# Attention scores: the low-key product with 64 rows of high query only, two heads in the two halves of the TensorE array

## The chip, the core and the metric

The kernel runs on one core of a Trainium2 chip. The metric is the device time of one launch in microseconds (us). Before the change the median of three runs is 2594.91 us (2594.48 to 2594.93).

## The reference

One encoder layer is applied to a prompt of 512 tokens and a sample of 256 tokens (width 2048), with shared weights. What the change touches is the windowed attention: 16 query heads of 64 channels in 4 groups, each group sharing one of 4 key/value heads, after a rotary turn. Each block of 128 queries sees its own key block and its neighbours.

```python
def window_attention(q, k, v, sink):
    ...
    scale = HEAD_DIM ** -0.5
    s = jnp.einsum('bnqhgd,bnkhd->bnhgqk', qb, kb).astype(jnp.float32) * scale
    ...
    s = jnp.where(valid[None, :, None, None, :, :], s, NEG_INF)
    m = jnp.maximum(jnp.max(s, axis=-1, keepdims=True), sink_l)
    p = jnp.exp(s - m)
    p = p / (jnp.sum(p, axis=-1, keepdims=True) + jnp.exp(sink_l - m))
    o = jnp.einsum('bnhgqk,bnkhd->bnqhgd', p.astype(v.dtype), vb)
```

Around it stand an RMSNorm and the input projection, a 2-D Fourier mix of the other 1024 channels, the output projection `w_out`, and a squared-ReLU MLP of width 8192.

## The kernel before

Every float32 product is made from two parts of each factor: a high part (the value as TensorE's one-pass float32 format, `F32R`, holds it) and a low part (the rest). A product is then high times high, high times low and low times high.

The program runs in stages: the input projection with the Fourier mix (to about 378 us of the trace), then a stage that interleaves the attention with the output projection (378 to about 735 us), then the two MLP products (lines 1187 and 1622), which fill the rest.

In the attention stage TensorE's order is written out by hand. The output projection is the ground beat: a step is one pass through `proj_slot` for one `k`, three matmuls of 512 columns (line 1040), and `run_events` is called after each step. The attention work is hung into this beat through a heap of events, `at(t, fn)`, with `t` in steps. TensorE's instructions are placed so, and the DMA issues on SP and the work of VectorE, ScalarE and GpSimd stand in the same order in their own queues.

The attention itself is cut into 24 units, `units[u] = (b, g)`: six query blocks `b` by four head groups `g`, with four heads `h` each. A unit begins every `pace` = 7.37 steps. For one head, `qk` (line 839) makes the scores `s` (128 queries by `nk` keys; `nk` is 256 in the 16 units of blocks 0, 3, 4 and 5, and 384 in the 8 units of blocks 1 and 2). `row_max` (VectorE, line 863) adds the mask, takes the maximum and writes the masked scores into `p`, which frees the PSUM buffer of `s`; there are three such buffers. Then come `exps` (ScalarE), `normalize` (GpSimd, line 893), `trans` (four transposes on TensorE, line 905) and `pv` (line 924).

A tile `qs` holds a unit's queries: rows 0 to 63 the high part, rows 64 to 127 the low part, for four heads. `kdh` and `kdl` hold the high and the low keys, each twice, in the upper and in the lower 64 rows. So one matmul with `kdh` over 128 rows gives (high + low query) times high key, and one with `kdl` gives (high + low query) times low key. That is two matmuls a head, 192 in all. The heads' events are `d_qk` = 1.73 steps apart; `row_max` follows 0.4 step after `qk`.

`load_q(u)` (line 724) brings `qs` from two scratch tensors in HBM, `qr_d[g][0]` (high) and `qr_d[g][1]` (low), with two DMA issues on SP. `qs` has two buffers, so the load for unit `u + 2` waits until the scores of unit `u` are done. Other issues on the same queue bring the weights of the output projection (`raw`) and the Fourier results (`ofr`).

Of the kernel before, what the change touches and what calls it, by code (L numbers as in the profile page):

```python
# [12 lines left out]
F32R = mybir.dt.float32r  # L13
# [7 lines left out]
P = 128  # L21
# [11 lines left out]
HD = 64  # L33
# [7 lines left out]
def hybrid_encoder(ctx: ExitStack, tc: tile.TileContext, a: dict):  # L41
    nc = tc.nc
    ctx.enter_context(tc.manual_schedule(engines={mybir.EngineType.PE}))

    def f32(ap):
        return ap.bitcast(F32)
# [71 lines left out]
    qr_d = [[dpool.tile([2 * P, T], F32, tag=f"q{c}{i}", name=f"q{c}{i}") for c in "hl"] for i in range(NKV)]  # L118
# [60 lines left out]
    def load_of(m, tiles=None):  # L179

        of_raw[m] = tiles or [
            op.tile([P, FG, P], F32, tag=f"of{'hl'[m - 1]}-1", name="ofr")
            if m < 3 else ap_.tile([P, FG, P], F32, tag="ofr", name="ofr", bufs=2)
        ]
        for i, raw in enumerate(of_raw[m]):
            k = raw.shape[1]
            src = of_d[i * k * P : (i + 1) * k * P, m * P : (m + 1) * P]
            nc.sync.dma_start(raw[:], src.rearrange("(k p) t -> p k t", p=P))
# [9 lines left out]
    with ExitStack() as ph:  # L198
# [456 lines left out]
        kt = {}  # L655
# [65 lines left out]
        units = [(b, g) for b in range(NM) for g in range(NKV)]  # L721
        state = {}

        def load_q(u):
            b, g = units[u]
            t0 = slice(b * P, (b + 1) * P)
            qs = kt["kp"].tile([P, 4, P], F32R, tag="qs", name="qs", bufs=2)
            state[u] = {"qs": qs}
            for o in range(2):
                nc.sync.dma_start(f32(qs[o * HD : (o + 1) * HD]), qr_d[g][o][:, t0].rearrange("(d h) t -> d h t", h=4))  # L730

        todo = {}

        def after(piece, fn):
            todo.setdefault(piece, []).append(fn)
# [20 lines left out]
            after(14.5 + i, lambda i=i: load_k(i))  # L756
        for u in range(2):
            after(18 + 0.5 * u, lambda u=u: load_q(u))
        after(18, lambda: load_of(0, [kt["kp"].tile([P, 4, P], F32, tag="zy", name="ofr", bufs=2) for _ in range(2)]))
        n_in = 4 * len(cols)  # L760
        in_raw, in_w = {}, {}
# [26 lines left out]
        for piece in range(n_in):  # L788
# [7 lines left out]
            for c in range(2):  # L796
                cs = slice(c * P, (c + 1) * P)
                for i in range(4):
                    first, stop = j == 0 and i == 0, j == 3 and i == 3
                    for w, o, n in ((wh, 0, 0), (wh, 1, 1), (wl, 0, 2)):  # L800
                        for s in range(2):
                            nc.tensor.matmul(  # L802
                                ps[c][s][:, :HALF], w[:, i, cs], whole[j // 2][s][o][:, 4 * (j % 2) + i, :],
                                start=first and n == 0, stop=stop and n == 2,
# [28 lines left out]
    mask, sink, kdh, kdl = (kt[c] for c in ("mask", "sink", "kdh", "kdl"))  # L833

    def key_blocks(b):
        lo, hi = (0, 3) if b < 4 else (4, 5)
        return max(lo, b - 1), min(hi, b + 1)

    def qk(u, heads):
        b, g = units[u]  # L840
        k0, k1 = key_blocks(b)
        nk = (k1 - k0 + 1) * P
        st = state[u]
        for h in heads:
            s = tiles.pop("s", None) or pp3.tile([P, 512], F32, tag="s", name="s", bufs=3)
            st[f"s{h}"] = s
            for n, kd in enumerate((kdl, kdh)):
                nc.tensor.matmul(s[:, :nk], st["qs"][:, h, :], kd[:, g, k0 * P : k0 * P + nk], start=(n == 0), stop=(n == 1))  # L848

    def row_max(u, heads):  # L850
        b, g = units[u]
        k0, k1 = key_blocks(b)
        nk = (k1 - k0 + 1) * P
        off = (k0 - b + 1) * P
        st = state[u]
        if heads[0] == 0:
            for x, w in (("mx", 4), ("nm", 4), ("rs", 4), ("es", 4), ("p", 4 * 384)):
                st[x] = ap_.tile([P, w], F32, tag=x, name=x)
            st["p"] = st["p"][:].rearrange("p (h k) -> p h k", h=4)
        mx = st["mx"]  # L860
        for h in heads:
            s = st[f"s{h}"]
            nc.vector.tensor_tensor_reduce(
                out=st["p"][:, h, :nk], in0=s[:, :nk], in1=mask[:, off : off + nk], scale=1.0,
                scalar=sink[:, 4 * g + h : 4 * g + h + 1], op0=ALU.add, op1=ALU.max, accum_out=mx[:, h : h + 1],
            )
        hs = slice(heads[0], heads[-1] + 1)
        nc.vector.tensor_scalar(out=st["nm"][:, hs], in0=mx[:, hs], scalar1=-1.0, scalar2=None, op0=ALU.mult)
        if heads[-1] == 3:
            nc.vector.tensor_tensor(out=st["es"][:], in0=sink[:, 4 * g : 4 * g + 4], in1=mx[:], op=ALU.subtract)  # L870

    def exps(u, heads):
        b, g = units[u]
        k0, k1 = key_blocks(b)
        nk = (k1 - k0 + 1) * P
        st = state[u]
        for h in heads:
            nc.scalar.activation(
                st["p"][:, h, :nk], st["p"][:, h, :nk], AF.Exp, bias=st["nm"][:, h : h + 1],
                accum_out=st["rs"][:, h : h + 1],  # L880
            )
        if heads[-1] == 3:
            nc.scalar.activation(st["es"][:], st["es"][:], AF.Exp)

    def normalize(u):
        k0, k1 = key_blocks(units[u][0])
        nk = (k1 - k0 + 1) * P
        st = state[u]
        rs, es, p = st["rs"], st["es"], st["p"]
        nc.vector.tensor_tensor(out=rs[:], in0=rs[:], in1=es[:], op=ALU.add)  # L890
        nc.vector.reciprocal(out=rs[:], in_=rs[:])
        for h in range(4):
            nc.gpsimd.tensor_scalar(
                out=p[:, h, :nk], in0=p[:, h, :nk], scalar1=rs[:, h : h + 1], scalar2=1.0, op0=ALU.mult, op1=ALU.mult
            )
        st["pt"] = {}

    def trans(u, kb):
        st = state[u]
        k0, k1 = key_blocks(units[u][0])  # L900
        if k0 + kb > k1:
            return
        pt = tiles.pop("t", None) or pp3.tile([P, 512], F32, tag="t", name="t", bufs=3)
        for h in range(4):
            nc.tensor.transpose(pt[:, h * P : (h + 1) * P], st["p"][:, h, kb * P : (kb + 1) * P], ident[:])  # L905
        th = ap_.tile([P, 512], F32R, tag="th", name="th", bufs=4)
        tl = ap_.tile([P, 512], F32R, tag="tl", name="tl", bufs=4)
        later(t_th, lambda: nc.scalar.activation(th[:], pt[:], AF.Copy))
        later(t_tl, lambda: nc.vector.tensor_tensor(out=tl[:], in0=pt[:], in1=f32(th[:]), op=ALU.subtract))
        st["pt"][kb] = (th, tl)  # L910
# [73 lines left out]
    pace, t_first, t_qk, d_qk, t_max, t_exp, t_norm = 7.37, 4, -4.5, 1.73, 0.4, 2.65, 3.65  # L984
# [6 lines left out]
    def at(t, fn):  # L991
        clock[1] += 1
        heapq.heappush(events, (t, clock[1], fn))
# [8 lines left out]

    for u in range(len(units)):
        t = pace * u + t_first
        for h in range(4):
            dt = t_qk + d_qk * h
            at(t + dt, lambda u=u, h=h: qk(u, (h,)))
            at(t + dt + t_max, lambda u=u, h=h: row_max(u, (h,)))
            at(t + dt + t_exp, lambda u=u, h=h: exps(u, (h,)))
        at(t + t_norm, lambda u=u: normalize(u))  # L1010
        if u + 2 < len(units):
            at(t + t_lq + 2 * (u == 1), lambda u=u: load_q(u + 2))
        for kb in range(3):
            at(t + t_trans + d_trans * kb, lambda u=u, kb=kb: trans(u, kb))
            at(t + t_pv + d_pv * kb, lambda u=u, kb=kb: pv(u, kb))
# [117 lines left out]
    units = [(0, g) for g in range(NG)] + [(1, g) for g in (NG - 1, *range(NG - 1))]  # L1133
# [672 lines left out]
```

## Time and profile before

| | us |
|---|---|
| median of the three runs | 2594.91 |
| the profiled execution, its own time | 2593.48 |
| span of that execution | 2591.6 |
| TensorE busy in the span | 2576.9 |
| VectorE busy | 1810.9 |
| ScalarE busy | 1124.4 |
| GpSimd busy | 266.3 |
| attention interleaved with the output projection, from the first to the last score matmul | 378.2 to 577.5 |

PE is the matmul side of TensorE and PEld its weight load, which runs beside it; DVE is VectorE, ACT ScalarE, POOL GpSimd, SP the queue that issues most DMAs. The length that the profile gives a matmul reaches past the start of the next one, since matmuls are pipelined. What a matmul costs in a row of matmuls is therefore read from start to start, here called its slot.

### The profile page before, as it was taken

What the parts mean: (1) busy time and instruction counts of PE and PEld (TensorE: products, weight loads), DVE (VectorE), ACT (ScalarE), POOL (GpSimd) and SP (SyncE); (2) the same over time, 40 slices, a digit from 0 to 9 for tenths busy, and PEclk for the clock granted to TensorE, in tenths of its full rate; (3) what the DMA queues carried; (4) which work ended last, traced back from release to release, by engine and by line L of the source; (5) the groups of instructions that cost most, each with busy time, mean ns of one, the idle gap of its engine ahead of it and who ended that gap; (6) DMA issues with size and microseconds to landing.
All of it is one profiled execution on the core that took longest, in us unless ns stands there. A gap on an engine that the chain in (4) does not pass through costs nothing.

```text
span 2591.6 us, 34972 instructions
## 1 busy us (share of the span) xinstructions
PE 2576.9 (99%) x13580; PEld 2359.3 (91%) x13580; DVE 1810.9 (70%) x2208; ACT 1124.4 (43%) x1574; POOL 266.3 (10%) x367
## 2 busy tenths in 40 slices
PE   9999999999999999999999999999999999999998
PEld 9999998888899999999999999988888888888887
DVE  7966567777655656556777877767776765777687
ACT  6545437674334333333444454433333333333335
POOL 1001333233210101000000000110000000000000
PEclk9999999999999999999999999999999999999999
DMA  7863385345664445456666766675543662555364
GB/s 251 311 225 113 127 240 175 117 131 193 216 202 159 163 157 187 161 191 236 212 216 227 232 215 213 240 306 176 184 153 112 219 235 82 179 179 164 98 207 155
DMA packets 268998, 489.54 MB, mean 189 GB/s; under 512 B 19568, under 2 KB 164000, under 8 KB 267424
## 3 DMA queue, kind: packets, MB, share of 16 engines
q1 hardware_dynamic: 197328, 321.26, 39.2%
q10 hardware_dynamic: 58688, 115.18, 11.7%
q0 software_dynamic: 12816, 50.87, 5.8%
q8 instruction: 107, 1.75, 0.3%
q14 instruction: 59, 0.48, 0.1%
HBM read 360.35 MB, written 126.88 MB: 188 GB/s over the span
## 4 chain that ended last, share of the span: by engine, by line
PE 96%; DVE 1%; DMA 1%; ACT 1%; issue 0%; POOL 0%; SPq 0%; DVEq 0%; POOLq 0%; ACTq 0%
PE pu L1187 36%; PE pd L1622 35%; PE pm L1040 10%; PE pz L802 5%; PE p L268 4%; PE o L924 1%; PE t L905 1%; PE s L848 1%; PE pv L391 1%; PE ptx L137 0%; PE pe L630 0%; PE pa L609 0%; DMA raw<-in_w_in 0%; DMA zf<-zf 0%; PE pt L137 0%
## 5 line engine op out<-in xcount | busy, mean ns | idle before, releaser
L1187 PE MATMUL pu<-xf,wh 128*128 128x384 f32 x3072 | 780.2, 334 | 0.0
L1187 PEld LDWEIGHTS pu<-xf,wh 128*128 128x128 f32 x3072 | 554.0, 188 | 1.5 <-ACT o L1205 1.3
L1622 PE MATMUL pd<-wl,sh 128*128 128x512 f32 x1332 | 517.7, 389 | 0.0
L1622 PE MATMUL pd<-wh,sh 128*128 128x512 f32 x1332 | 517.7, 389 | 0.0
L1622 PE MATMUL pd<-wh,sl 128*128 128x512 f32 x1332 | 517.5, 389 | 0.0
L1187 PE MATMUL pu<-xf,wl 128*128 128x384 f32 x1536 | 513.1, 334 | 0.0
L1599 ACT ACTIVATE wh<-rd 128x1024 fp32r<-128x1024 f32 x200 | 202.5, 1054 | 522.4 <-PE pd L1622 421.8
L1609 DVE TENSOR_TENSOR wl<-rd,wh 128x1024 fp32r<-128x1024 f32 x200 | 236.0, 1221 | 226.6 <-ACT wh L1599 225.9
L1167 ACT ACTIVATE wh<-ur 128x1024 fp32r<-128x1024 f32 x160 | 170.1, 1063 | 382.6 <-PE pu L1187 214.4
L1622 PEld LDWEIGHTS pd<-wh,sh 128*128 128x128 f32 x1332 | 250.0, 188 | 51.9
L1622 PEld LDWEIGHTS pd<-wh,sl 128*128 128x128 f32 x1332 | 249.9, 188 | 52.0 <-DVE sl L1610 0.3
L1622 PEld LDWEIGHTS pd<-wl,sh 128*128 128x128 f32 x1332 | 250.0, 188 | 51.7
L1187 PEld LDWEIGHTS pu<-xf,wl 128*128 128x128 f32 x1536 | 288.3, 188 | 0.0
L1173 DVE TENSOR_TENSOR wl<-ur,wh 128x1024 fp32r<-128x1024 f32 x160 | 195.4, 1221 | 76.2 <-ACT wh L1167 76.1
L1208 DVE TENSOR_TENSOR o<-pu,o 128x768 f32<-128x768 f32 x160 | 152.8, 956 | 122.5 <-PE pu L1187 114.9
L1592 DVE TENSOR_TENSOR rd<-rd 128x1024 f32<-128x1024 f32 x112 | 131.7, 1217 | 0.0
L1187 PE MATMUL pu<-xs,wh 128*128 128x384 f32 x512 | 129.8, 334 | 0.0
L1167 ACT ACTIVATE wh<-sx 128x1024 fp32r<-128x1024 f32 x64 | 67.9, 1062 | 130.5 <-PE pu L1187 99.4
L268 PE MATMUL p<-xs,wh 128*128 128x384 f32 x448 | 113.7, 334 | 0.0
L1610 DVE TENSOR_TENSOR sl<-sr,sh 128x768 fp32r<-128x768 f32 x111 | 105.5, 951 | 0.0
L101 POOL TENSOR_TENSOR ry<-ry,mhalf 128x1 f32<-128x1 f32 x5 | 5.5, 1099 | 871.8 <-DVE ry L98 871.8
L1173 DVE TENSOR_TENSOR wl<-sx,wh 128x1024 fp32r<-128x1024 f32 x64 | 78.2, 1222 | 23.8 <-ACT wh L1167 23.6
(278 smaller groups left out, 4017.3 us busy)
## 6 DMA issues: line engine op xcount, KB each, us to landing
rd<-in_w_down SPq DMA_DIRECT2D x176, 512.0 KB, 5.2
ur<-in_w_up SPq DMA_DIRECT2D x128, 512.0 KB, 3.9
sr<-sd SPq DMA_DIRECT2D x95, 384.0 KB, 5.3
pd<-o ACTq DMA_DIRECT2D x60, 384.0 KB, 2.3
o<-pd POOLq DMA_DIRECT2D x60, 384.0 KB, 6.0
sd<-sm ACTq DMA_DIRECT2D x60, 384.0 KB, 2.7
raw<-in_w_in SPq DMA_DIRECT2D x38, 512.0 KB, 6.3
raw<-in_w_out SPq DMA_DIRECT2D x32, 512.0 KB, 4.6
```

The lines of the kernel that those rows point to most:

```text
L268: nc.tensor.matmul(ps7[bank, g, r][:, :HALF], l[:, i, r * P : (r + 1) * P], x[:, o, 4 * e + i, :], start=(opens and e == 0 and i == 0 and ...
L802: nc.tensor.matmul(ps[c][s][:, :HALF], w[:, i, cs], whole[j // 2][s][o][:, 4 * (j % 2) + i, :], start=first and n == 0, stop=stop and n == 2,)
L1040: nc.tensor.matmul(ps, l(k), w[:, k % 2, :], start=(k == 0 and n == 0), stop=(k == 7 and n == 2))
L1167: nc.scalar.activation(wh[:], raw[:], AF.Copy)
L1173: nc.vector.tensor_tensor(out=wl[:], in0=raw[:], in1=f32(wh[:]), op=ALU.subtract)
L1187: nc.tensor.matmul(ps[:, t, :HALF], w[:, i, t * P : (t + 1) * P], xb[:, o, i, :], start=(s == first_of[bank] and i == 0 and n == 0), stop= ...
L1208: nc.vector.tensor_tensor(out=o, in0=src, in1=o, op=ALU.add)
L1592: add = lambda x, y, op: nc.vector.tensor_tensor(out=x[:], in0=x[:], in1=y[:], op=op)
L1599: nc.scalar.activation(wh[:], t[:], AF.Copy)
L1609: nc.vector.tensor_tensor(out=wl[:], in0=t[:], in1=f32(wh[:]), op=ALU.subtract)
L1610: nc.vector.tensor_tensor(out=sl[:], in0=sr[:], in1=f32(sh[:]), op=ALU.subtract)
L1622: nc.tensor.matmul(o, l[:, q, ts], w[:, ns], start=(j == j0 and (q, t) == (0, 0)), stop=(j == j1 and (q, t) == (1, 2)),)
```

## The change

Per pair of heads there were four matmuls over 128 rows. There are now two over 128 rows (with `kdh`) and two over 64 rows (with `kdl`). The product of the low query with the low key is no longer computed. The two 64-row products of a pair go into the upper half of the array (`tile_position=(0, 0)`) and into its lower half (`(64, 0)`), into two PSUM buffers.

[...] There `qs` holds low query parts, so a new tile `qx0` or `qx1` (one buffer each) is filled in its lower half with the high query part of the pair's second head, by one more DMA issue on SP for each pair, 48 in all. The pairs are heads (0, 2) and (1, 3). The first unit's two loads are issued before the stage; the others one step after the pair that last read the tile.

```diff
             qs = kt["kp"].tile([P, 4, P], F32R, tag="qs", name="qs", bufs=2)
-            state[u] = {"qs": qs}
+            state.setdefault(u, {})["qs"] = qs
...
+        def load_high(u, i):
+            if u == len(units):
+                return
+            b, g = units[u]
+            qx = state.setdefault(u, {})[f"qx{i}"] = kt["kp"].tile([P, P], F32R, tag=f"qx{i}", name=f"qx{i}")
+            src = qr_d[g][0][:, b * P : (b + 1) * P].rearrange("(d h) t -> d h t", h=4)
+            nc.sync.dma_start(f32(qx[HD:]), src[:, 2 + i])
...
             after(18 + 0.5 * u, lambda u=u: load_q(u))
+            after(18, lambda i=u: load_high(0, i))
...
+        ks = slice(k0 * P, k0 * P + nk)
         for h in heads:
             s = tiles.pop("s", None) or pp3.tile([P, 512], F32, tag="s", name="s", bufs=3)
             st[f"s{h}"] = s
-            for n, kd in enumerate((kdl, kdh)):
-                nc.tensor.matmul(s[:, :nk], st["qs"][:, h, :], kd[:, g, k0 * P : k0 * P + nk], start=(n == 0), stop=(n == 1))
+            nc.tensor.matmul(s[:, :nk], st["qs"][:, h, :], kdh[:, g, ks], start=True, stop=False)
+        h0, h1 = heads
+        nc.tensor.matmul(st[f"s{h0}"][:, :nk], st["qs"][:HD, h0, :], kdl[:HD, g, ks], start=False, stop=True, tile_position=(0, 0))
+        nc.tensor.matmul(st[f"s{h1}"][:, :nk], st[f"qx{h0}"][HD:], kdl[HD:, g, ks], start=False, stop=True, tile_position=(HD, 0))
...
-        for h in range(4):
-            dt = t_qk + d_qk * h
-            at(t + dt, lambda u=u, h=h: qk(u, (h,)))
+        for i, h in enumerate((0, 2, 1, 3)):
+            dt = t_qk + d_qk * i
+            if i % 2 == 0:
+                at(t + dt, lambda u=u, h=h: qk(u, (h, h + 2)))
+                at(t + dt + 1, lambda u=u, h=h: load_high(u + 1, h))
             at(t + dt + t_max, lambda u=u, h=h: row_max(u, (h,)))
             at(t + dt + t_exp, lambda u=u, h=h: exps(u, (h,)))
```

How TensorE's order moves is seen in a unit with 384 keys (block 1, group 0). Before, the first and the second head's scores (`s_4440` and `s_4476` are their PSUM tiles) stand apart, with transposes (`t`) of the unit before and two steps of the output projection (`pm`) between them:

```order
L848 MATMUL s_4440<-kdl_3370,qs_4326 128x384
L848 MATMUL s_4440<-kdh_3369,qs_4326 128x384
L905 MATMUL t_4443<-ident_65,p_4256 128x128 x4
L1040 MATMUL pm_4377<-wh_4097,ofh3_4056 128x512
L1040 MATMUL pm_4377<-wl_4098,ofh3_4056 128x512
L1040 MATMUL pm_4377<-wh_4097,ofl3_4057 128x512
L1040 MATMUL pm_4377<-wh_4097,ofh3_4056 128x512
L1040 MATMUL pm_4377<-wl_4098,ofh3_4056 128x512
L1040 MATMUL pm_4377<-wh_4097,ofl3_4057 128x512
L848 MATMUL s_4476<-kdl_3370,qs_4326 128x384
L848 MATMUL s_4476<-kdh_3369,qs_4326 128x384
L1040 MATMUL pm_4480<-wh_3898,ofh4_4058 128x512
```

In the changed program the same place reads:

```order
L1054 MATMUL pm_4398<-wh_4007,ofl3_4061 128x512
L857 MATMUL s_4460<-kdh_3369,qs_4342 128x384
L857 MATMUL s_4462<-kdh_3369,qs_4342 128x384
L859 MATMUL s_4460<-kdl_3370,qs_4342 128x384
L860 MATMUL s_4462<-kdl_3370,qx0_4394 128x384
L917 MATMUL t_4466<-ident_65,p_4271 128x128 x4
L1054 MATMUL pm_4398<-wh_4103,ofh3_4060 128x512
L1054 MATMUL pm_4398<-wl_4104,ofh3_4060 128x512
```

The pair's second head (`s_4462`, head 2 of the unit) now stands right behind the first. The last two of the four score matmuls are the 64-row ones, and behind the last one the array goes back to 128 rows. Two PSUM tiles are taken at once.

On SP, in the same units, `qs` (two issues a unit) and `raw` stood alone before:

```order
L79 DMA raw_4354<-in_w_out 128x2x512
L730 DMA qs_4422<-qh1_84 64x4x128
L730 DMA qs_4422<-ql1_85 64x4x128
L162 DMA raw_4433<-in_w_out 128x2x512
L730 DMA qs_4518<-qh2_86 64x4x128
L730 DMA qs_4518<-ql2_87 64x4x128
```

Now there are two `qx` issues a unit between them:

```order
L79 DMA raw_4373<-in_w_out 128x2x512
L738 DMA qx0_4394<-qh0_82 64x128
L738 DMA qx1_4428<-qh0_82 64x128
L730 DMA qs_4442<-qh1_84 64x4x128
L730 DMA qs_4442<-ql1_85 64x4x128
L162 DMA raw_4453<-in_w_out 128x2x512
L738 DMA qx0_4494<-qh1_84 64x128
L738 DMA qx1_4525<-qh1_84 64x128
```

Each `qx` issue waits for the pair one unit earlier, which read the same tile, and `qs` and `raw` stand behind that wait.

## Prediction

> **What bounds the kernel now.** I read the page first: the span, TensorE's share, and the chain of waits by engine.
>
> ```profile
> span 2591.6 us, 34972 instructions
> PE 2576.9 (99%) x13580; PEld 2359.3 (91%) x13580; DVE 1810.9 (70%) x2208; ACT 1124.4 (43%) x1574; POOL 266.3 (10%) x367
> PE 96%; DVE 1%; DMA 1%; ACT 1%; issue 0%; POOL 0%; SPq 0%; DVEq 0%; POOLq 0%; ACTq 0%
> ```
>
> TensorE is the bound, so a slot saved or added on it is time. Then the busy time in stretches of the attention stage (columns: PE, PEld, DVE, ACT, POOL, granted clock, DMA share, GB/s), and the chain of waits in that stage.
>
> ```profile
> 390.00:400.00 10.00, 7.62 (x33) 5.87 (x33) 8.40 (x26) 6.61 (x17) 4.37 (x5) 0.83 0.68 224
> 400.00:450.00 50.00, 50.00 (x263) 42.59 (x262) 38.32 (x113) 36.68 (x87) 14.02 (x24) 1.00 0.60 182
> 390.42 4.02 POOL p L893 x4
> ```
>
> From 400 us on TensorE has no gap. Before that, up to 394.5 us, the chain runs through VectorE and the first unit's normalization on GpSimd. What TensorE gains or loses ahead of 394.5 us does not count as long as its idle time there lasts.
>
> **What a score matmul costs.** The groups by shape, and single matmuls in a unit of 384 keys (start, recorded length):
>
> ```profile
> L848 PE MATMUL s<-kdh,qs 128*128 128x256 f32 x64 | 18.1, 284 | 0.0
> L848 PE MATMUL s<-kdl,qs 128*128 128x256 f32 x64 | 18.0, 282 | 0.0
> L848 PE MATMUL s<-kdl,qs 128*128 128x384 f32 x32 | 10.9, 341 | 0.0
> 442.04 0.33 PE L848 MATMUL s<-kdl,qs 128*128 128x384 f32 x1
> 442.21 0.34 PE L848 MATMUL s<-kdh,qs 128*128 128x384 f32 x1
> 442.39 0.40 PE L1040 MATMUL pm<-wh,ofh 128*128 128x512 f32 x1
> ```
>
> The recorded 0.34 us is not the cost: the next start comes after 0.17 to 0.18. The chain of waits gives slots over longer runs, and a third number, matmuls of one column, where nothing but the weight load can set the pace:
>
> ```profile
> 219.20 1.43 PE pe L630 x12
> 297.76 4.17 PE pz L802 x24
> 301.93 1.38 PE ps_r L648 x12
> ```
>
> A slot of 256 columns is 1.43/12 = 0.119 us, one of 384 is 4.17/24 = 0.174, and a weight load needs 1.38/12 = 0.115.
>
> **What is saved.** 48 pairs lose one slot each if the two 64-row products run side by side, none if they run one after the other. Four pairs (units 0 and 1, 256 keys) lie ahead of 394.5 us. That leaves 28 of 256 and 16 of 384 keys: 28 x 0.119 + 16 x 0.174 = 6.1 us at most. But both halves still bring a load of their own. No row of before has 64 rows; if these loads take 0.115 and follow each other like all others, the second half starts 0.115 behind the first, and a pair saves only slot minus load: 28 x 0.004 + 16 x 0.059 = 1.1 us. Bounds 0 to 6.1. I take 1.1, since every row has one load behind another.
>
> **What the switch of the array costs.** No row shows a switch between 128 and 64 rows. The nearest is the array leaving the transposes of line 905:
>
> ```profile
> 439.88 0.60 PE L905 MATMUL t<-ident,p 128*128 128x128 f32 x4
> 440.24 0.42 PE L848 MATMUL s<-kdl,qs 128*128 128x384 f32 x1
> 440.50 0.33 PE L848 MATMUL s<-kdh,qs 128*128 128x384 f32 x1
> 440.66 0.40 PE L1040 MATMUL pm<-wh,ofh 128*128 128x512 f32 x1
> ```
>
> The score matmul behind the transposes holds 0.26 us instead of 0.174, so this switch costs 0.086. Going in costs nothing that can be seen (four transposes in 0.36 us). For the upper end, a load that is not hidden: the four matmuls of line 1042, once in the flow and once behind a real wait.
>
> ```profile
> 380.66 1.07 PE L1042 MATMUL pm<-wh,ofl 128*128 128x512 f32 x4
> 387.36 1.20 PE L1042 MATMUL pm<-wh,ofl 128*128 128x512 f32 x4
> ```
>
> That is 0.13 us for one uncovered load. If the array must also run empty first, add the recorded length less the slot, 0.284 - 0.119 = 0.165. So one switch costs 0 to 0.295 us. There are two for each pair, 88 that count: 0 to 26.0 us. I take the transposes' 0.086: 7.6 us.
>
> [...]
>
> **Loads, waits, buffers.** The 48 new issues take SP about what those of `qs` take, 0.52 us each, some 25 us over 200 us. SP mostly waits there, and the loads land in about 3 us:
>
> ```profile
> qs<-qh SPq DMA_DIRECT2D x24, 128.0 KB, 2.9
> SPq L730 <- PE s L848: 63.6, 11, 7.7
> 444.98 1.37 PE o L924 x6
> 453.94 1.37 PE o L924 x6
> 392.31 0.52 SPq L730 DMA_DIRECT2D qs<-qh  x1
> ```
>
> A unit is 453.94 - 444.98 = 9.0 us for 7.37 steps, 1.22 a step. A `qx` load is placed 6.37 steps ahead of its reader, 7.8 us against 2.9: hidden. Without that cover a late load would hold all of TensorE, up to 3 us a pair. Behind the new wait on SP stand `qs` and `raw`; SP waited for the same scores before, the unit's last scores now come 1.73 steps earlier, and `raw` has two buffers. I cost it at 0.
>
> Two score buffers of three are taken at once. Pair two of a unit needs the first head's maximum of the same unit, 3.06 steps or 3.7 us earlier, in place of 4.8 steps before. That is covered where VectorE keeps up, but not in units 0 and 1:
>
> ```profile
> 385.26 0.47 DVE L863 CUSTOM_DVE_ANT_0 p<-s,mask,sink 128x256 f32<-128x256 f32 x1
> 388.16 0.19 PEld L848 LDWEIGHTS s<-kdl,qs 128*128 128x128 f32 x1
> 389.28 0.48 DVE L863 CUSTOM_DVE_ANT_0 p<-s,mask,sink 128x256 f32<-128x256 f32 x1
> 391.22 0.33 PE L905 MATMUL t<-ident,p 128*128 128x128 f32 x1
> 392.09 0.78 PE L905 MATMUL t<-ident,p 128*128 128x128 f32 x2 [0.54 <-POOL p L893]
> 394.48 0.48 PE L905 MATMUL t<-ident,p 128*128 128x128 f32 x1 [1.61 <-POOL p L893]
> 384.81 0.28 PE L848 MATMUL s<-kdl,qs 128*128 128x256 f32 x1
> ```
>
> Unit 1's first pair (384.8) must wait for the third maximum (to 385.7), and its second (388.2) for the maximum of 389.3: 0.9 + 1.5 = 2.4 us. The transposes wait over 2 us for GpSimd anyway, and VectorE's chain does not hang on these scores, so TensorE's idle time only moves. Cost 0; 2.4 us if GpSimd were not late.
>
> **Sum.** 2593.48 - 1.1 + 7.6 = 2600.0 for an execution like the profiled one. The median of the runs is 1.43 above that, so 2601.4 against 2594.91. Its own range, from half to one and a half of the switch cost, is 2597.6 to 2605.2.
>
> **Rivals.**
> 1. *Side by side, and the switch is free.* The loads of the two halves go together and nothing drains: 2594.91 - 6.1 = 2588.8. For it: PEld is hidden in every slot of this stage, and the transposes are entered at no cost. Against it: leaving them does cost. [...]
> 2. *The array drains at every switch.* 88 x 0.165 = 14.5, less 1.1: 2608.3; with the load uncovered too, 26.0 less 1.1: 2619.8. It decides from a price of 0.07 a switch on, where 6.1 us of saving are eaten up. For it: the two kinds of score matmul need other rows of the array, so a load ahead may be barred. Against it: the transposes' exit costs only half a drain.
> 3. *It cancels, or the halves do not run together and the switch is free.* Full saving with the transposes' price gives 7.6 - 6.1 = +1.5, 2596.4; no saving and no price 2594.9.
>
> **How the numbers follow.** The forecast gets 0.38, rival 1 0.17, rival 2 0.23, rival 3 0.22. This measurement can tell about 0.2% from no change, 5.2 us. Faster by more: rival 1 nearly whole, 0.15. Same: rival 3, and the lower part of the forecast, 0.29. Slower: the upper part of the forecast and rival 2, 0.56. The range runs from rival 1 to where rival 2 is mostly taken in, 2589 to 2617.
>
> **What would show it.** Starts in the steady part (400 to 577 us), from a pair's first matmul to the next matmul behind the pair, at 256 keys: four slots before, 0.48 us. Forecast 0.24 + 0.23 + 0.17 = 0.64; rival 1 0.36; rival 2 0.80 to 1.06. [...] Line 1187 and line 1622 must keep their shares. The prediction falls if TensorE waits for `qx`, if the gaps at `s` tiles reach past 400 us, or if the 394.5 us of the first transposes moves.

## The result, and the profile after

The changed kernel takes 2603.25 us (median of 7 runs, 2602.13 to 2605.57) against 2594.93 for the kernel before on the same chip (7 runs). The ratio is 1.0032, 95% interval 1.0023 to 1.0041: 8.3 us slower. The page of the changed kernel:

```profile
span 2600.2 us, 35049 instructions
PE 2586.0 (99%) x13580; PEld 2354.3 (91%) x13580; DVE 1808.7 (70%) x2208; ACT 1125.6 (43%) x1574; POOL 266.2 (10%) x367
PE 98%; DVE 1%; DMA 0%; ACT 0%; issue 0%; ACTq 0%; DVEq 0%; POOLq 0%; POOL 0%; SPq 0%
```

TensorE's busy time grew by 9.1 us with the same count of matmuls, and the span by 8.6. The last row of the chain of waits that matters is the start of the first long MLP row (before, then after):

```profile
735.06 8.35 PE pu L1187 x48
743.97 8.35 PE pu L1201 x48
```

It is 8.9 us later, so the loss lies in the attention stage or ahead of it, and the MLP gives 0.3 back. The groups of the score matmuls by shape show the 64-row form (`64*128`):

```profile
L857 PE MATMUL s<-kdh,qs 128*128 128x256 f32 x64 | 13.5, 285 | 1.3 <-DVE mx L875 1.3
L859 PE MATMUL s<-kdl,qs 64*128 64x256 f32 x32 | 12.2, 381 | 0.0
L860 PE MATMUL s<-kdl,qx 64*128 64x256 f32 x32 | 12.2, 381 | 0.0
```

The recorded length of a 64-row product is 381 ns where a full one had 283, for half the rows: a first sign that something beside the product is in it. One pair in the steady part shows what. First TensorE's matmuls, in order of time (start, recorded length; x2 stands for two merged into one row), then the weight loads of the same place:

```profile
509.59 0.40 PE L857 MATMUL s<-kdh,qs 128*128 128x256 f32 x2
509.92 0.38 PE L859 MATMUL s<-kdl,qs 64*128 64x256 f32 x1
509.92 0.38 PE L860 MATMUL s<-kdl,qx 64*128 64x256 f32 x1
510.23 0.49 PE L1054 MATMUL pm<-wh,ofh 128*128 128x512 f32 x1
510.56 0.39 PE L1054 MATMUL pm<-wl,ofh 128*128 128x512 f32 x1
```

```profile
509.37 0.41 PEld L857 LDWEIGHTS s<-kdh,qs 128*128 128x128 f32 x2
509.92 0.18 PEld L859 LDWEIGHTS s<-kdl,qs 64*128 64x128 f32 x1
509.92 0.18 PEld L860 LDWEIGHTS s<-kdl,qx 64*128 64x128 f32 x1
510.23 0.19 PEld L1054 LDWEIGHTS pm<-wh,ofh 128*128 128x128 f32 x1
510.34 0.19 PEld L1054 LDWEIGHTS pm<-wl,ofh 128*128 128x128 f32 x1
```

Read start to start. Two full matmuls hold 0.33 us where two slots are 0.24: 0.09 passes before the array takes the halves. Both halves start at the same time, and so do their two loads. The next matmul starts 0.31 later, where a slot is 0.119, and itself holds 0.33 us where 0.23 is usual. In the flow a load starts while the matmul before it runs (the load of L857 at 509.37, its matmul at 509.59). At the switch it starts together with its own matmul, both on the way in (509.92) and on the way out (510.23): it is not hidden, and the load after it follows 0.11 later (510.34), near the 0.115 that the prediction reads for one load. So in all the pair takes 0.33 + 0.31 us, and 0.10 of extra time in the next matmul, 0.74 us, against four slots of 0.119 before, 0.48.

### The profile page after: what moved, and what is told of

It reads as the page before. It is cut to its first block, busy times and chain, and to the rows that moved or that the text cites. A ratio compares the mean times of both kernels' runs of the same rounds, so it can differ in the third digit from the quotient of the medians.

```text
span 2600.2 us, 35049 instructions
## 1 busy us (share of the span) xinstructions
PE 2586.0 (99%) x13580; PEld 2354.3 (91%) x13580; DVE 1808.7 (70%) x2208; ACT 1125.6 (43%) x1574; POOL 266.2 (10%) x367
## 4 chain that ended last, share of the span: by engine, by line
PE 98%; DVE 1%; DMA 0%; ACT 0%; issue 0%; ACTq 0%; DVEq 0%; POOLq 0%; POOL 0%; SPq 0%
PE pu L1201 36%; PE pd L1636 35%; PE pm L1054 10%; PE pz L811 6%; PE p L268 4%; PE pv L391 1%; PE t L917 1%; PE o L936 1%; PE s L859 1%; PE s L857 0%; PE ptx L137 0%; PE pa L609 0%; PE pe L630 0%; DMA raw<-in_w_in 0%; PE pt L137 0%
```

## The experiments

Three theories stood against each other. A: the halves run side by side and save a slot, but each pair pays some 0.38 us for going into the 64-row form and out again. B: the halves run one after the other and the switch is cheap. C: not the array but the new order costs the time (pairs, two score buffers at once, the `qx` loads).

**The new order with full rows.** Both low-key products of a pair over 128 rows again.

```diff
-        h0, h1 = heads
-        nc.tensor.matmul(st[f"s{h0}"][:, :nk], st["qs"][:HD, h0, :], kdl[:HD, g, ks], ..., tile_position=(0, 0))
-        nc.tensor.matmul(st[f"s{h1}"][:, :nk], st[f"qx{h0}"][HD:], kdl[HD:, g, ks], ..., tile_position=(HD, 0))
+        for h in heads:
+            nc.tensor.matmul(st[f"s{h}"][:, :nk], st["qs"][:, h, :], kdl[:, g, ks], start=False, stop=True)
```

> The changed kernel with the same order, the same pairs and the same 48 loads of qx, but both low-key products of a pair over 128 rows again (qx is loaded and not read). Theory A (the switch between 128 and 64 rows costs about 0.38 us a pair and the halves save one slot): back near before, 2592 to 2598 us. Theory B (the halves run one after the other, 0.155 us each, and the switch is cheap): also near before. Theory C (the pairs, the two score buffers at once and the qx loads cost the time): stays near 2603 us.

Measured: 2594.41 us (11 runs), ratio to before 0.9998, 0.9989 to 1.0007. Theory C falls: the order, the buffers and 48 more loads cost nothing that the runs can tell. The same place in this trace has four plain slots, 0.47 us from the first score to the next `pm`:

```profile
506.68 0.40 PE L857 MATMUL s<-kdh,qs 128*128 128x256 f32 x2
506.91 0.40 PE L859 MATMUL s<-kdl,qs 128*128 128x256 f32 x2
507.15 0.40 PE L1053 MATMUL pm<-wh,ofh 128*128 128x512 f32 x1
507.38 0.40 PE L1053 MATMUL pm<-wl,ofh 128*128 128x512 f32 x1
```

**One half alone.** The second head's 64-row product is left out.

```diff
-            nc.tensor.matmul(s[:, :nk], st["qs"][:, h, :], kdh[:, g, ks], start=True, stop=False)
+            nc.tensor.matmul(s[:, :nk], st["qs"][:, h, :], kdh[:, g, ks], start=True, stop=(h == heads[1]))
...
-        nc.tensor.matmul(st[f"s{h1}"][:, :nk], st[f"qx{h0}"][HD:], kdl[HD:, g, ks], start=False, stop=True, tile_position=(HD, 0))
```

> The changed kernel without the 64-row product of each pair's second head (the low-key product of heads 2 and 3 is left out). Theory A: the second half runs beside the first and was free, so the time stays at 2602 to 2604 us. Theory B: 44 pairs lose 0.15 us each, 2596 to 2597 us. Theory C: stays near 2603 us.

Measured: 2603.74 us (5 runs), ratio 1.0033, 1.0020 to 1.0046, the same as the changed kernel. Theory B falls: the second half is free. In the trace one half holds the same 0.31 us as two:

```profile
510.54 0.40 PE L857 MATMUL s<-kdh,qs 128*128 128x256 f32 x2
510.87 0.38 PE L859 MATMUL s<-kdl,qs 64*128 64x256 f32 x1
511.18 0.50 PE L1053 MATMUL pm<-wh,ofh 128*128 128x512 f32 x1
511.51 0.40 PE L1053 MATMUL pm<-wl,ofh 128*128 128x512 f32 x1
```

**Both halves in the upper half of the array.**

```diff
-        nc.tensor.matmul(st[f"s{h1}"][:, :nk], st[f"qx{h0}"][HD:], kdl[HD:, g, ks], ..., tile_position=(HD, 0))
+        nc.tensor.matmul(st[f"s{h1}"][:, :nk], st["qs"][:HD, h1, :], kdl[:HD, g, ks], ..., tile_position=(0, 0))
```

> The changed kernel with both 64-row products of a pair in the upper half of the array, from the high query part in rows 0 to 63 (qx is loaded and not read); the same values are computed. Theory A: they can't run side by side, so one slot comes back, 28 x 0.119 + 16 x 0.174 = 6.1 us, about 2609 us, up to 2614 if the second load isn't hidden either. Theory B: they were one after the other before, so no change, 2603 us. Theory C: no change.

Measured: 2609.30 us (5 runs), ratio 1.0055, 1.0042 to 1.0068; that is 6.05 us over the changed kernel, and 6.1 was expected. So the full slot is what running side by side saves; in the trace a pair of 256 keys takes 0.12 us longer than in the changed kernel, one of 384 keys 0.17. The trace also takes the switch apart (matmuls, then loads):

```profile
510.60 0.39 PE L857 MATMUL s<-kdh,qs 128*128 128x256 f32 x2
510.93 0.38 PE L859 MATMUL s<-kdl,qs 64*128 64x256 f32 x1
511.15 0.28 PE L860 MATMUL s<-kdl,qs 64*128 64x256 f32 x1
511.36 0.66 PE L917 MATMUL t<-ident,p 128*128 128x128 f32 x4
```

```profile
510.92 0.18 PEld L859 LDWEIGHTS s<-kdl,qs 64*128 64x128 f32 x1
511.03 0.19 PEld L860 LDWEIGHTS s<-kdl,qs 64*128 64x128 f32 x1
511.36 0.42 PEld L917 LDWEIGHTS t<-ident,p 128*128 128x128 f32 x4
```

The first half holds 0.22 us: its own load, 0.11, and a slot. The second one's load starts at 511.03, when by this reading the first half begins to run, and is hidden behind it although both use the same 64 rows: the second half starts 0.12 us after that load. The second holds 0.21, a slot and 0.09 until the array is taken by the next form. So one switch is two things: about 0.09 us in which nothing new starts, and one load of 0.11 that does not run ahead. Going in and out costs 0.09 + 0.11 + 0.09 + 0.10 = 0.39 us; the last term is the load on the way out, as the plain matmul behind the pair shows it. What passes in the array during the 0.09 us the profile does not show.

**A switch for each head.** The kernel before, in its own order, with the low-key product over 64 rows for every head alone.

```diff
-            for n, kd in enumerate((kdl, kdh)):
-                nc.tensor.matmul(s[:, :nk], st["qs"][:, h, :], kd[:, g, k0 * P : k0 * P + nk], start=(n == 0), stop=(n == 1))
+            ks = slice(k0 * P, k0 * P + nk)
+            nc.tensor.matmul(s[:, :nk], st["qs"][:, h, :], kdh[:, g, ks], start=True, stop=False)
+            nc.tensor.matmul(s[:, :nk], st["qs"][:HD, h, :], kdl[:HD, g, ks], start=False, stop=True, tile_position=(0, 0))
```

> The kernel before, in its own order and without qx, with each head's low-key product over the upper 64 rows only: two switches for each head in place of two for each pair, and no partner beside it. Theory A: 88 heads x 0.38 us = 33.7 us over before, about 2628 us. Theory B: 88 x (0.155 - 0.119), about 2598 us. Theory C: as before, 2595 us.

Measured: 2625.91 us (4 runs), ratio 1.0120, 1.0106 to 1.0134; 31.0 us over before, where theory A had 33.7 and the others 3 or nothing. Twice the switches and no partner: this is the price by itself, 31.0/88 = 0.35 us for each head that the prediction counts. In the trace a head takes 0.39 us more than before where a plain matmul follows and 0.34 where transposes follow; over the 84 heads from unit 3 on that adds up to 31.5.

**One switch for four heads.** In the 16 units of 256 keys all scores of a unit are made at one place, with two heads in one score buffer.

```diff
+        if nk == 256:
+            if heads[0] != 0:
+                return
+            for i in (0, 2):
+                s = tiles.pop("s", None) or pp3.tile([P, 512], F32, tag="s", name="s", bufs=3)
+                for j in range(2):
+                    st[f"s{i + j}"] = s[:, j * nk : (j + 1) * nk]
+            pairs = ((0, 2), (1, 3))
...
+        for hs in pairs:
+            for h in hs:
+                nc.tensor.matmul(st[f"s{h}"], st["qs"][:, h, :], kdh[:, g, ks], start=hs is pairs[0], ...)
+        for h0, h1 in pairs:
+            for h, x, c in ((h0, st["qs"][:HD, h0, :], 0), (h1, st[f"qx{h0}"][HD:], HD)):
+                nc.tensor.matmul(st[f"s{h}"], x, kdl[c : c + HD, g, ks], start=False, stop=True, ..., tile_position=(c, 0))
```

> The changed kernel, but in the 16 units of 256 keys all four heads' scores are made at one place: four 128-row products, then two pairs of 64-row products behind one switch (heads 0 and 1 share one score buffer, heads 2 and 3 another). The units of 384 keys stay as they are. Theory A, with the price as measured so far (0.38 us a pair for going in and out, 44 pairs that count): 14 units lose one of two switches, 14 x 0.38 = 5.3 us, about 2598 us; still above before, since two slots saved, 0.24 us, do not pay for one 0.38. If the price were for each 64-row product and not for the switch, or for the loads of qx: no change, 2603 us.

Measured: 2607.93 us (5 runs), ratio 1.0049, 1.0035 to 1.0063: a miss, slower than the changed kernel where 2598 was expected. The waits of TensorE (us in total, times, longest) and one of the places name the reason; in brackets stands the idle time before a matmul and what ended it:

```profile
PE s L871 <- DMA qx<-qh: 5.0, 3, 2.5
501.23 0.28 PE L871 MATMUL s<-kdl,qs 64*128 64x256 f32 x1
504.01 0.58 PE L871 MATMUL s<-kdl,qx 64*128 64x256 f32 x1 [2.51 <-DMA qx<-qh]
508.42 0.63 PE L1065 MATMUL pm<-wh,ofl 128*128 128x512 f32 x1
508.85 0.63 PE L1065 MATMUL pm<-wh,ofh 128*128 128x512 f32 x1
```

The second pair had moved 3.46 steps ahead, and the load of its `qx1` had not. TensorE waited three times (until 409.37, 504.01 and 565.11 us). Behind the longest wait, 2.51 us, matmuls of 512 columns came 0.43 us apart in place of 0.23, from 505.86 to 510.13 us, and the granted clock was 0.93 over 500 to 550 us; behind the two others, 0.73 and 1.79 us, they stayed at 0.23, with a granted clock of 1.00 from 410 to 450 and from 550 to 600 us. This says nothing of the switch, so the load was moved too.

**The same, with the load in time.**

```diff
-                at(t + dt + 1, lambda u=u, h=h: load_high(u + 1, h))
+                at(t + (dt if units[u][0] in (1, 2) else t_qk) + 1, lambda u=u, h=h: load_high(u + 1, h))
```

> The kernel of the experiment before (one switch for each unit of 256 keys), with the load of qx1 moved as far ahead as that of qx0, behind the place where both are read. In the run before, TensorE waited three times for qx, 5.0 us in all, and ran at the low clock behind each wait. Theory A (the price belongs to the switch): the waits are gone and 14 units save one of two switches, 14 x 0.38 = 5.3 us against the changed kernel, 2597 to 2599 us. If the price belongs to each 64-row product: 2603 us. If the waits for qx are not what cost the time in the run before: still near 2608 us.

Measured: 2597.55 us (11 runs), ratio 1.0010, 1.0001 to 1.0019; 5.7 us under the changed kernel (5.3 when each is set against the kernel before as it was timed beside it, 8.3 and 3.0 us over it), 5.3 expected. So the price is for the switch, not for the 64-row product, and the waits for `qx` with what followed them are what the run before had lost. The low clock, though, had followed one of its three waits and not each. A unit of 256 keys in this trace:

```profile
520.14 0.64 PE L868 MATMUL s<-kdh,qs 128*128 128x256 f32 x4
520.71 0.38 PE L871 MATMUL s<-kdl,qs 64*128 64x256 f32 x1
520.71 0.38 PE L871 MATMUL s<-kdl,qx 64*128 64x256 f32 x1
520.93 0.28 PE L871 MATMUL s<-kdl,qs 64*128 64x256 f32 x1
520.94 0.28 PE L871 MATMUL s<-kdl,qx 64*128 64x256 f32 x1
521.14 0.66 PE L928 MATMUL t<-ident,p 128*128 128x128 f32 x4
```

The second pair of halves adds 0.22 - 0.11 = 0.11 us, a plain slot, and no switch. Still, two slots saved are 0.24 us and the round trip costs more, so this kernel stays behind the one before. An estimate of what is left: the 16 pairs of 384 keys still make a round trip each and lose 16 x 0.19 = 3.0 us, and 14 units of 256 keys lose about 0.1 each (0.35 ahead of transposes less 0.24), 1.4; the 3.0 us measured have an interval of 0.3 to 4.9. By these numbers a switch comes out even with three pairs of 256 keys ahead of transposes (3 x 0.119 = 0.36 against 0.35) and pays from four pairs on in either place (0.48 against 0.39). Four pairs need four score buffers of two heads each; there are three, and it was not tried.

## Why the prediction came out as it did

The forecast was 2601.4 us with 2589 to 2617 around it, and slower. The time, 2603.25, and the direction agree. That the time comes within 1.8 us is luck: two terms of the sum were off by more than the sum was, the saving by 5 us and the price by 7 to 9, with opposite effect. What held is that TensorE sets the pace and that the price of the switch is above the saving. The sign that was named for a pair of 256 keys, 0.64 us from its first matmul to the next matmul behind it, was met too (0.33 + 0.31), by the same luck: the second half starts 0.00 us behind the first and not 0.115, and 0.10 us more falls into the matmul behind the pair, which that sum leaves out.

- *What is saved.* The sum took 1.1 us, with the halves' loads one behind the other. They start at the same time, and so do the halves; the experiment in one half of the array puts the saving at 6.05 us, the upper end (6.1). This part of rival 1 came true. Between the two starts lie 0.00 to 0.01 us, in the changed kernel (509.92 both) as in the last experiment (520.93 and 520.94).
- *What the switch costs.* The sum took 0.086 us a switch, from the transposes, 7.6 us in all. It is 0.17 to 0.19 (0.35 to 0.39 for in and out), so 88 x 0.17 to 0.19 = 15 to 17 us. The rows of the transposes show no price of a switch. Their weight loads follow each other by 0.11 us, and so does the load of the score behind them:

```profile
439.88 0.36 PEld L905 LDWEIGHTS t<-ident,p 128*128 128x128 f32 x3
440.21 0.19 PEld L848 LDWEIGHTS s<-kdl,qs 128*128 128x128 f32 x1
440.32 0.19 PEld L848 LDWEIGHTS s<-kdh,qs 128*128 128x128 f32 x1
```

  Four loads of 0.108 and a slot of 0.174 are 0.61 us, and the four transposes with the score matmul hold 0.36 + 0.26 = 0.62. So the 0.086 that the score matmul has too much is what the four transposes have too little; they go at the pace of their loads.

  The price found lies inside the bounds of 0 to 0.295, and its two parts are those named for the upper end: an uncovered load (0.13 taken, 0.11 found, 0.06 where transposes follow) and a stop before it (0.165 taken for an array that runs empty, 0.09 found). The recorded length of a matmul less its slot overstates the second. The mean of the bounds, 0.15, would have been nearer than the transposes. That the array runs empty at a switch was a supposition, and no run shows it; what the traces show is 0.09 us at each change in which nothing new starts, and the load on top.
- *The sum.* From 402 us on, where TensorE sets the pace in both, the distance between the changed kernel and the same order with full rows grows by 9.5 us over 42 pairs (0.25 a pair of 256 keys, 0.19 one of 384, each start to start: 26 x 0.25 + 16 x 0.19 = 9.5). Against the kernel before it grows by 9.1, from 0.2 us ahead at 402 us to the 8.9 behind at the MLP. The prediction counted 44 pairs; those of unit 2 stand ahead of 402 us and were set off there (see the clock, below).
- *Ahead of 394.5 us.* That the first four pairs do not count was right: the wait for GpSimd ends at 393.99 us in place of 394.48, and the first score had started 0.5 us earlier too. At the first product `o`, behind unit 2, the changed kernel is level with the one before (before, then after):

```profile
402.19 0.40 PE L924 MATMUL o<-th,vhl 128*128 128x512 f32 x1
402.02 0.39 PE L936 MATMUL o<-th,vhl 128*128 128x512 f32 x1
```

  Two waits for score buffers came in unit 1 as foreseen, but short, 0.16 and 0.25 us where 0.9 and 1.5 were reckoned. A third, in unit 2, was not foreseen, and came behind the transposes:

```profile
385.32 0.38 PE L857 MATMUL s<-kdh,qs 128*128 128x256 f32 x1 [0.16 <-DVE mx L875]
389.33 0.39 PE L857 MATMUL s<-kdh,qs 128*128 128x256 f32 x1 [0.25 <-DVE mx L875]
393.99 0.33 PE L917 MATMUL t<-ident,p 128*128 128x128 f32 x1 [1.35 <-POOL p L905]
397.37 0.28 PE L857 MATMUL s<-kdh,qs 128*128 128x256 f32 x1
398.55 0.39 PE L857 MATMUL s<-kdh,qs 128*128 128x256 f32 x1 [0.90 <-DVE mx L875]
```

- *The clock there.* In the stretch from 390 to 400 us the granted clock is 1.00, where it was 0.83. Before, matmuls of 512 columns behind the wait for GpSimd started 0.42 us apart (395.19 and 395.61 us) in place of 0.23, at a granted clock of 0.50 from 394 to 396 us; from the starts up to 397.6 us I estimate that this had cost some 1.3 us. The changed kernel does not pay it, and that about makes up for the third wait and for the 0.5 us that unit 2's two pairs lose. The sum had a term for none of the three; that they cancel is luck. Why the clock stayed up is not shown: in the last experiment a wait of the same 1.61 us ends at 394.73 us, and the matmuls of 512 columns behind it start 0.24 and 0.23 us apart from 395.13 us on.

```profile
390.00:400.00 10.00, 7.75 (x40) 5.76 (x39) 8.43 (x25) 6.99 (x17) 4.77 (x6) 1.00 0.70 223
```

- *Loads.* No matmul waited for `qx`, as costed. The price named if the cover were gone, up to 3 us a pair, is what the fifth experiment ran into (0.73 to 2.51 us, with matmuls 0.43 us apart behind the longest).
- *The rivals.* Neither came whole. The outcome is the saving of rival 1 with a price at the low end of rival 2's, 15 to 17 us of 14.5 to 26.0. The third, that it cancels, was wrong by the same switch.

## What to carry to other kernels

Packing two 64-row products into the array saves one whole slot here (6.05 us in the runs, 0.12 us a pair of 256 keys), but by these numbers that pays only where the array stays in that form for a while: going in and out costs 0.35 to 0.39 us, as much as three slots of 256 columns (0.36). Count the round trips and not the products, and gather as many packed products behind one switch as the score buffers allow. One pair and two pairs of 256 columns were tried and lose; by these numbers it takes four to gain. Before a price is borrowed from another place, add that place up with its neighbours: the transposes and the matmul behind them together held no switch. When a piece of work is moved ahead, move the load that feeds it too.

## What the runs showed of the hardware that was not expected

A weight load into the same 64 rows that the running matmul uses is hidden behind it (load at 511.03 us, the running half's own start about then, the next start at 511.15); at a change of form, in these traces, the load starts only with its own matmul (509.92 and 510.23 us in the changed kernel, 510.92 and 511.36 with both halves in the upper half). And a switch into the transposes from the 64-row form costs 0.06 us on top of them (0.41 us for four in place of 0.36) where one into a plain matmul costs 0.10, so a pair placed right ahead of transposes is the cheaper one (0.35 against 0.39 us for in and out). In the fifth experiment matmuls of 512 columns came 0.43 us apart after a wait of 2.51 us for `qx` (from 505.86 to 510.13 us), and after one of 1.60 us for GpSimd (from 398.25 to 399.11 us, granted clock 0.88 from 390 to 400 us); after waits of 0.73 and 1.79 us in the same trace they came 0.23 apart. What sets this is not shown.
